# Linear attention in a hybrid decoder trunk: the chunk state of four heads packed into one 64-column block

## The chip, the cores and the metric

One core of one Trainium2 chip. The time is the device time of one execution in microseconds; three runs of the kernel before gave 1186.64, 1187.30 and 1189.42 us, median 1187.3. The profile is of one execution of its own, which took 1187.23 us.

## The reference

Two layers over 512 tokens of 1024 channels. Each layer normalises, projects to four mixers (latent attention, gated linear attention, block attention, a gated recurrence), concatenates, projects back, and runs a SwiGLU network of 2816 hidden channels. The change lies in the gated linear attention: four heads, keys of 32 and values of 64 channels, eight chunks of 64 tokens.

```
b = cumsum(log_sigmoid(a_low @ w_a2 + b_a2) / 16)        # in each chunk
att     = (qf * exp(b - b_last/2)) @ (kf * exp(b_last/2 - b)).T   # 64x64, causal
o_intra = att @ vf
d_state = (kf * exp(b_last - b)).T @ vf                  # 32x64 for head and chunk
state   = exp(b_last) * state + d_state                  # from chunk to chunk
o_inter = (qf * exp(b)) @ state_before
y       = rms_norm(o_intra + o_inter) * silu(g)
```

## The kernel before

Activations lie channels by tokens, 128 x 512 a tile. The dense products run in split single precision: each weight tile and each activation is cut into a high and a low part (`whi`, `wlo`, `xhi`, `xlo`), and a product is three matmuls of 128 x 128 by 128 x 512 (`mm3`). Their outputs are the PSUM tiles `pd` (channels by tokens) and `pt` (tokens by channels). A weight tile comes by DMA into `raw`, ScalarE copies it to `whi`, VectorE or GpSimd subtracts to give `wlo` (`load_split`). Layer 1's mixer weights are split during layer 0's feed-forward and kept in DRAM (`ahead`).

The program is first recorded as a list of operations. A planner in the kernel (`Recorder.schedule`) then lists them in one order by priority, due time and its own cost figures, gives out buffer slots, and that order is emitted; each engine works through its own in that order. `gate` and `also` add a predecessor, or buffers to be had at once, to what is recorded inside them; they bear on the plan alone, and the waits on the chip come from the data. `packed(n)` divides an operation's planned cost by n. `unbroken` makes a run of matmuls start only when the inputs of all are there, and go out in one piece. The dense products have the lowest priority (50), so they fill TensorE whenever nothing else is due.

The linear attention is in two functions. `gla_gates` makes the decays `dcy`, the gated `qt`, `kt`, `qh` (in `gq`'s buffer) and `kh`, the scores `ps_a` (four heads, each 32 rows of the array, four PSUM banks), their masked form `am`, and `khT`, keys by channels. `gla_outputs` does the rest. The state before the change has 256 columns: 128 rows are four heads of 32 channels, columns are four heads of 64 values, and only the four diagonal blocks of 32 x 64 are used. `st` is eight such blocks in four tiles, set to zero by GpSimd. For each pair of chunks, two matmuls (64 rows each, `ps_d`) give the whole 128 x 256 product, and for each chunk and head VectorE adds one 32 x 64 block to the decayed block before (`scalar_tensor_tensor`, 28 in a layer with the first chunk's copies). For each pair of heads, `ps_og` collects eight matmuls of the scores (128 rows, 64 columns of the array, two heads beside one another) and then seven of 128 x 128 state columns by 64 tokens of `qh`, where the zeros in `st` keep the heads apart. ScalarE copies and squares each of the two `ps_og`. A float32 matmul stands in the trace as two instructions, so that 7 matmuls are 14 rows, 16 are 32.

In the profile all recorded operations carry line 397, so tiles are told apart by name.

Of the kernel before, what the change touches and what calls it, by code (L numbers as in the profile page):

```python
# [15 lines left out]
ALU = mybir.AluOpType  # L16
# [3 lines left out]
P = 128  # L20
# [4 lines left out]
QT = S // P  # L25
# [4 lines left out]
NCHUNK = S // CH  # L30
# [370 lines left out]
def trunk_kernel(ctx: ExitStack, tc: tile.TileContext, io):  # L401
    nc = tc.nc
    R = Recorder(nc)
    pe, act, dve, pool, sp = R.pe, R.act, R.dve, R.pool, R.sp
# [4 lines left out]
    def t512(group, dtype=F32, name="t", shape=(S,)):  # L409
        return R.buf("sbuf", group, shape, dtype, name)  # L410
# [4 lines left out]
    def psum(group, name="ps"):  # L415
        return R.buf("psum", group, (S,), F32, name)

    def f(v):
        return v.bitcast(F32)

    def mm(out, l, r, start, stop, **kw):
        return pe.matmul(out, l, r, start=start, stop=stop, skip_group_check=True, **kw)
# [88 lines left out]
    def load_split(ap, group="w", key=None, issue=None):  # L511
        if key in ahead:
            with prio(P_LOAD):
                n = ap.shape[-1]
                hi, lo = t512(group, F32R, "whi", (n,)), t512(group, F32R, "wlo", (n,))
                chain = loads.setdefault(group, [])
                with also(lo), gate(turn["att" if group == "att" else "w"], *chain[-6:-5]):
                    first_ = sp.dma_start(f(hi), ahead[key][0])
                with gate(first_):
                    chain.append(sp.dma_start(f(lo), ahead[key][1]))  # L520
            return hi, lo
        with prio(P_LOAD):
            n = ap.shape[-1]
            raw = t512("raw", F32, "raw", (n,))
            chain = loads.setdefault(group, [])
            with gate(*chain[-6:-5]):
                chain.append((issue or sp).dma_start(raw, ap))
            hi, lo = t512(group, F32R, "whi", (n,)), t512(group, F32R, "wlo", (n,))
            with also(lo):
                act.copy(hi, raw)  # L530
            dve.tensor_sub(lo, raw, f(hi))
        return hi, lo

    class Weights:
# [5 lines left out]
        def block(self, i):  # L540
            if i // 4 != self.at:
                self.at = i // 4
                c = slice(self.at * S, min((self.at + 1) * S, self.n))
                self.w = load_split(self.ap[:, c], self.group, (self.key, self.at))
            c = slice(i % 4 * P, (i % 4 + 1) * P)
            return self.w[0][:, c], self.w[1][:, c]
# [20 lines left out]
    def with_x(k):  # L567
        if k == 0:
            first[0] += [load_split(io["w_in0"][0, 0][:, P:])]
        else:  # L570
            first.append([load_split(io["w_in0"][0, k])])
# [29 lines left out]
    def rstd(ps, n, dim):  # L601
        v, y, t, r = (tiny(name=c)[:, :n] for c in "vytr")
        dve.tensor_scalar(v, ps, 1.0 / dim, EPS, op0=ALU.mult, op1=ALU.add)
        pool.tensor_tensor(y, v, negh[:, :n], op=ALU.pow)
        dve.scalar_tensor_tensor(t, y, -0.5, y, op0=ALU.mult, op1=ALU.mult)
        dve.tensor_mul(t, t, v)
        dve.scalar_tensor_tensor(r, t, 1.5, y, op0=ALU.add, op1=ALU.mult)
        return r
# [365 lines left out]
        return att, khT, qh, dcy, last  # L974

    def gla_outputs(v, att, khT, qh, dcy, last):
        st = []
        with gate(last):
            for _ in range(NCHUNK // 2):
                t = t512("seq", name="st", shape=(2, 256))  # L980
                pool.memset(t, 0.0)
                st += [t[:, 0], t[:, 1]]
        for c0 in range(0, NCHUNK - 1, 2):
            pds = {c: psum("m", "ps_d")[:, :256] for c in (c0, c0 + 1) if c < NCHUNK - 1}
            with unbroken():
                for c, pd in pds.items():
                    r = slice(64 * (c % 2), 64 * (c % 2) + 64)
                    with also(*pds.values()), packed(len(pds)):
                        mm(pd, khT[r, (c // 2) * P:(c // 2 + 1) * P], v[c // 2][r, :], True, True,
                           tile_position=(64 * (c % 2), 0))  # L990
            for c, pd in pds.items():
                for h in range(4):
                    hr, hv = slice(32 * h, 32 * h + 32), slice(64 * h, 64 * h + 64)
                    if c == 0:
                        dve.tensor_copy(st[1][hr, hv], pd[hr, hv])
                    else:
                        dve.scalar_tensor_tensor(st[c + 1][hr, hv], st[c][hr, hv], dcy[hr, c, :], pd[hr, hv],
                                                 op0=ALU.mult, op1=ALU.add)
        os, sqs = [], []
        for p in range(2):  # L1000
            po = psum("m", "ps_og")
            with unbroken():
                for t, hh in ((t, hh) for t in range(QT) for hh in range(2)):
                    tt = slice(t * P, (t + 1) * P)
                    h = 2 * p + hh
                    with packed(2, 19.0):
                        mm(po[64 * hh:64 * hh + 64, tt], v[t][:, h * 64:(h + 1) * 64], att[h][:, tt], t == 0, False)
            for c in range(1, NCHUNK):
                cc = slice(c * CH, (c + 1) * CH)
                mm(po[:, cc], st[c][:, p * P:(p + 1) * P], qh[:, cc], False, c == NCHUNK - 1)  # L1010
            o, sq = t512("seq", name="og"), t512("seq", name="sqg")
            act.copy(o, po)
            act.activation(sq, po, AF.Square)
            os.append(o)
            sqs.append(sq)
        pn = psum("m", "ps_gn")
        for p in range(2):
            for t in range(QT):
                i = 2 * (p * QT + t)
                mm(pn[:, i:i + 2], sqs[p][:, t * P:(t + 1) * P], hsel, True, True)  # L1020
        return os, rstd(pn[:, :16], 16, 64)
# [94 lines left out]
    for l in range(L):  # L1116
# [29 lines left out]
        for what in ORDER:  # L1146
            if what == "v":
                dense_tm([io["w_tm"][l, 0, c] for c in range(4)], nrm, ev_v, "v")
                with prio(9):
                    gla = gla_outputs(gv, *gla)  # L1150
                    gla_end = R.ops[-1]
            elif what == "qk":
                dense_tm([io["w_tm"][l, 1, c] for c in range(4)], nrm, ev_qk, "qk")
            else:
                i = 2 * ("rx", "sg", "rg").index(what)
                fm[what] = [scaled(dense_fm(wf[i + m], nrm, f"fm{i + m}"), nrm, what) for m in range(2)]
# [29 lines left out]
        last = l == L - 1  # L1186
# [9 lines left out]
        for half in range(2):  # L1196
# [16 lines left out]
            with prio(P_DENSE):  # L1213
# [15 lines left out]
                if tail:  # L1229
                    c0 = (KT - tail) * HH * P  # L1230
                    ws = [load_split(io["w_fo"][l, half][:, c:min(c + S, KT * HH * P)], "h")
                          for c in range(c0, KT * HH * P, S)]
                    for q in range(2):
                        c = slice(256 * q, 256 * q + 256)
# [119 lines left out]
```

## Time and profile before

| | |
|---|---|
| median of three runs | 1187.3 us |
| profiled execution | 1187.23 us |
| its span, first to last instruction | 1185.5 us |
| around the span | 1.7 us |
| mean granted TensorE clock | 0.996 |
| busy: TensorE, VectorE, ScalarE, GpSimd | 1168.1, 684.9, 531.6, 232.8 us |
| `ps_d` instructions on TensorE | 28, in 7 pieces |
| `ps_og` instructions on TensorE | 64 of scores, 56 of states |
| state steps on VectorE | 48 steps and 8 copies |

A timeline row gives the start, the time until the last of the merged instructions ends, the engine, the operation with its output and inputs, the stationary tile as rows x columns, the moving operand, and how many instructions are merged. Matmuls are pipelined, so the rows overlap: what a matmul takes of TensorE is the distance between starts, not its duration.

### The profile page before, as it was taken

What the parts mean: (1) busy time and instruction counts of PE and PEld (TensorE: products, weight loads), DVE (VectorE), ACT (ScalarE), POOL (GpSimd) and SP (SyncE); (2) the same over time, 40 slices, a digit from 0 to 9 for tenths busy, and PEclk for the clock granted to TensorE, in tenths of its full rate; (3) what the DMA queues carried; (4) which work ended last, traced back from release to release, by engine and by line L of the source; (5) the groups of instructions that cost most, each with busy time, mean ns of one, the idle gap of its engine ahead of it and who ended that gap; (6) DMA issues with size and microseconds to landing.
All of it is one profiled execution on the core that took longest, in us unless ns stands there. A gap on an engine that the chain in (4) does not pass through costs nothing.

```text
span 1185.5 us, 16334 instructions
## 1 busy us (share of the span) xinstructions
PE 1168.1 (99%) x5568; PEld 963.1 (81%) x5568; DVE 684.9 (58%) x1249; ACT 531.6 (45%) x977; POOL 232.8 (20%) x217
## 2 busy tenths in 40 slices
PE   9999999999999999999999999999999999999996
PEld 6788878788888888888878788888888888888886
DVE  6867688776654456555523765777545433445422
ACT  6545876654443344434422477455433222333331
POOL 4524354460100000022204302206100000000011
PEclk9999999999999999999999999999999999999999
DMA  6322204258676777666795235643233333333312
GB/s 220 111 63 67 72 19 143 80 171 283 227 235 211 242 255 237 222 207 204 256 331 161 79 116 169 195 143 104 93 100 96 97 98 98 98 98 98 95 48 71
DMA packets 101618, 175.25 MB, mean 148 GB/s; under 512 B 11296, under 2 KB 21920, under 8 KB 101536
## 3 DMA queue, kind: packets, MB, share of 16 engines
q1 hardware_dynamic: 100704, 173.58, 46.0%
q8 instruction: 44, 0.72, 0.3%
q10 hardware_dynamic: 832, 0.63, 0.2%
q14 instruction: 38, 0.31, 0.1%
HBM read 139.04 MB, written 35.13 MB: 147 GB/s over the span
## 4 chain that ended last, share of the span: by engine, by line
PE 95%; DMA 1%; ACT 1%; DVE 1%; issue 1%; POOL 0%; POOLq 0%; SPq 0%; DVEq 0%; ACTq 0%
PE pd L397 77%; PE pt L397 8%; PE ps_s L397 2%; PE ps_pt L397 1%; PE ps_o L397 1%; PE ps_q L397 1%; PE ps_og L397 1%; DVE wlo L397 1%; PE ps_g L397 1%; PE ps_d L397 0%; DMA raw<-w_fm 0%; DMA wlo<-ahead 0%; DMA x<-xT 0%; ACT whi L397 0%; PE ps_k L397 0%
## 5 line engine op out<-in xcount | busy, mean ns | idle before, releaser
L397 ACT CAST whi<-raw 128x512 fp32r<-128x512 f32 (+2 forms) x330 | 201.5, 613 | 419.1 <-PE pd L397 376.7
L397 PE MATMUL pd<-xhi,wlo 128*128 128x512 f32 x896 | 350.1, 391 | 1.1 <-DMA wlo<-ahead 1.1
L397 PE MATMUL pd<-xlo,whi 128*128 128x512 f32 x896 | 350.6, 392 | 0.1
L397 PE MATMUL pd<-xhi,whi 128*128 128x512 f32 x896 | 349.0, 391 | 1.2 <-ACT whi L397 1.2
L397 DVE TENSOR_TENSOR wlo<-raw,whi 128x512 fp32r<-128x512 f32 (+2 forms) x282 | 211.8, 754 | 189.5 <-ACT whi L397 178.4
L397 PEld LDWEIGHTS pd<-xhi,wlo 128*128 128x128 f32 x896 | 168.3, 188 | 37.0 <-DMA wlo<-ahead 1.6
L397 PEld LDWEIGHTS pd<-xhi,whi 128*128 128x128 f32 x896 | 168.3, 188 | 37.0 <-ACT whi L397 2.5
L397 PEld LDWEIGHTS pd<-xlo,whi 128*128 128x128 f32 x896 | 168.2, 188 | 35.7 <-issue 1.5
L397 PE MATMUL pd<-hsh,whi 128*128 128x512 f32 (+1 forms) x374 | 141.1, 377 | 0.0
L397 PE MATMUL pd<-hsh,wlo 128*128 128x512 f32 (+1 forms) x374 | 141.0, 377 | 0.0
L397 PE MATMUL pd<-hsl,whi 128*128 128x512 f32 (+1 forms) x374 | 141.0, 377 | 0.0
L397 POOL TENSOR_TENSOR sq<-sq 128x512 f32<-128x512 f32 x35 | 51.1, 1460 | 352.0 <-ACT sq L397 349.9
L397 POOL TENSOR_TENSOR wlo<-raw,whi 128x512 fp32r<-128x512 f32 (+2 forms) x48 | 62.7, 1310 | 118.6 <-ACT whi L397 108.7
L397 PEld LDWEIGHTS pd<-hsh,wlo 128*128 128x128 f32 x374 | 70.3, 188 | 12.9
L397 PEld LDWEIGHTS pd<-hsh,whi 128*128 128x128 f32 x374 | 70.3, 188 | 12.9
L397 PEld LDWEIGHTS pd<-hsl,whi 128*128 128x128 f32 x374 | 70.3, 188 | 12.8
L397 DVE TENSOR_TENSOR x<-x,pd 128x512 f32<-128x512 f32 (+1 forms) x66 | 43.3, 668 | 51.0 <-PE pd L397 50.8
L397 POOL TENSOR_TENSOR plo<-praw,phi 128x512 fp32r<-128x512 f32 (+1 forms) x15 | 19.8, 1322 | 250.8 <-ACT phi L397 137.1
L397 DVE TENSOR_TENSOR fu<-pd,rbc 128x512 f32<-128x512 f32 x44 | 30.4, 691 | 52.3 <-PE pd L397 49.7
L397 DVE TENSOR_TENSOR fg<-pd,rbc 128x512 f32<-128x512 f32 x44 | 30.4, 690 | 40.8 <-PE pd L397 39.3
L397 PE MATMUL pt<-whi,xlo 128*128 128x512 f32 x128 | 51.0, 398 | 0.0
L397 PE MATMUL pt<-wlo,xhi 128*128 128x512 f32 x128 | 50.9, 398 | 0.0
(258 smaller groups left out, 1568.3 us busy)
## 6 DMA issues: line engine op xcount, KB each, us to landing
raw<-w_gu SPq DMA_DIRECT2D x176, 256.0 KB, 2.7
raw<-w_fo SPq DMA_DIRECT2D x88, 256.0 KB, 2.7
ahead<-phi SPq DMA_DIRECT2D x54, 256.0 KB, 3.2
ahead<-plo SPq DMA_DIRECT2D x54, 256.0 KB, 3.3
whi<-ahead SPq DMA_DIRECT2D x54, 256.0 KB, 2.7
wlo<-ahead SPq DMA_DIRECT2D x54, 256.0 KB, 3.2
x<-xT SPq DMA_DIRECT2D x16, 256.0 KB, 5.0
raw<-w_fm SPq DMA_DIRECT2D x16, 256.0 KB, 2.6
```

Of the source, the lines that this page charges most:

```text
L397: op.fn(*[r(a) for a in op.args], **{k: r(v) for k, v in op.kw.items()})
```

## The change

`st` becomes one tile of eight chunks by 64 columns, rows being the four heads' channels, so that each head holds only its own block and nothing has to be zero. The memsets go. The chunk products are made per head: 28 matmuls of 64 rows by 32 columns of the array (`tile_position` of row 0 or 64, column 0, 32, 64 or 96), even chunks into one PSUM bank and odd chunks into another, all in one unbroken run that starts after `khT` and all four value tiles. The recurrence takes the four heads in one VectorE instruction of 128 x 64, seven in a layer. The outputs of both pairs of heads are one unbroken run: 16 score matmuls as before, and then for each chunk four matmuls of 32 rows by 64 columns, one for each head. Last, in `load_split`, the planned copy of a weight tile to `whi` gets the DMA of the load before it as a further predecessor.

```diff
-            with also(lo):
+            with also(lo), gate(*chain[-2:-1]):
                 act.copy(hi, raw)
...
     def gla_outputs(v, att, khT, qh, dcy, last):
-        st = []
-        with gate(last):
-            for _ in range(NCHUNK // 2):
-                t = t512("seq", name="st", shape=(2, 256))
-                pool.memset(t, 0.0)
-                st += [t[:, 0], t[:, 1]]
-        for c0 in range(0, NCHUNK - 1, 2):
-            pds = {c: psum("m", "ps_d")[:, :256] for c in (c0, c0 + 1) if c < NCHUNK - 1}
-            with unbroken():
-                for c, pd in pds.items():
-                    r = slice(64 * (c % 2), 64 * (c % 2) + 64)
-                    with also(*pds.values()), packed(len(pds)):
-                        mm(pd, khT[r, (c // 2) * P:(c // 2 + 1) * P], v[c // 2][r, :], True, True,
-                           tile_position=(64 * (c % 2), 0))
-            for c, pd in pds.items():
+        st = t512("seq", name="st", shape=(NCHUNK, 64))
+        pds = [psum("m", "ps_d") for _ in range(2)]
+        with gate(last), unbroken():
+            for c in range(NCHUNK - 1):
+                r = slice(64 * (c % 2), 64 * (c % 2) + 64)
                 for h in range(4):
-                    hr, hv = slice(32 * h, 32 * h + 32), slice(64 * h, 64 * h + 64)
-                    if c == 0:
-                        dve.tensor_copy(st[1][hr, hv], pd[hr, hv])
-                    else:
-                        dve.scalar_tensor_tensor(st[c + 1][hr, hv], st[c][hr, hv], dcy[hr, c, :], pd[hr, hv],
-                                                 op0=ALU.mult, op1=ALU.add)
-        os, sqs = [], []
-        for p in range(2):
-            po = psum("m", "ps_og")
-            with unbroken():
-                for t, hh in ((t, hh) for t in range(QT) for hh in range(2)):
-                    tt = slice(t * P, (t + 1) * P)
-                    h = 2 * p + hh
-                    with packed(2, 19.0):
-                        mm(po[64 * hh:64 * hh + 64, tt], v[t][:, h * 64:(h + 1) * 64], att[h][:, tt], t == 0, False)
+                    hc = slice(c // 2 * P + 32 * h, c // 2 * P + 32 * h + 32)
+                    with also(*pds), packed(8):
+                        mm(pds[c % 2][32 * h:32 * h + 32, c // 2 * 64:c // 2 * 64 + 64], khT[r, hc],
+                           v[c // 2][r, h * 64:(h + 1) * 64], True, True, tile_position=(64 * (c % 2), 32 * h))
+        for c in range(NCHUNK - 1):
+            pd = pds[c % 2][:, c // 2 * 64:c // 2 * 64 + 64]
+            if c == 0:
+                dve.tensor_copy(st[:, 1], pd)
+            else:
+                dve.scalar_tensor_tensor(st[:, c + 1], st[:, c], dcy[:, c, :], pd, op0=ALU.mult, op1=ALU.add)
+        pos = [psum("m", "ps_og") for _ in range(2)]
+        with unbroken():
+            for t in range(QT):
+                tt = slice(t * P, (t + 1) * P)
+                for h in range(4):
+                    with also(*pos), packed(2, 19.0):
+                        mm(pos[h // 2][64 * (h % 2):64 * (h % 2) + 64, tt], v[t][:, h * 64:(h + 1) * 64], att[h][:, tt],
+                           t == 0, False)
             for c in range(1, NCHUNK):
                 cc = slice(c * CH, (c + 1) * CH)
-                mm(po[:, cc], st[c][:, p * P:(p + 1) * P], qh[:, cc], False, c == NCHUNK - 1)
+                for h in range(4):
+                    hr = slice(32 * h, 32 * h + 32)
+                    with packed(4):
+                        mm(pos[h // 2][64 * (h % 2):64 * (h % 2) + 64, cc], st[hr, c], qh[hr, cc], False, c == NCHUNK - 1,
+                           tile_position=(32 * h, 64 * (h % 2)))
+        os, sqs = [], []
+        for po in pos:
             o, sq = t512("seq", name="og"), t512("seq", name="sqg")
```

## Rows read from the trace of the kernel before

**Rows 1.** The page: busy time by engine (share, instructions), and the chain by engine.

```profile
PE 1168.1 (99%) x5568; PEld 963.1 (81%) x5568; DVE 684.9 (58%) x1249; ACT 531.6 (45%) x977; POOL 232.8 (20%) x217
PE 95%; DMA 1%; ACT 1%; DVE 1%; issue 1%; POOL 0%; POOLq 0%; SPq 0%; DVEq 0%; ACTq 0%
```

**Rows 2.** Timeline, TensorE, layer 1: one `ps_d` piece between dense matmuls.

```profile
656.13 0.39 PE L397 MATMUL ps_q<-cqh,wlo 128*128 128x512 f32 x1
656.36 0.40 PE L397 MATMUL ps_q<-cqh,whi 128*128 128x512 f32 x1
656.68 0.70 PE L397 MATMUL ps_d<-gv,khT 64*128 64x256 f32 x4
...
657.65 0.40 PE L397 MATMUL ps_q<-cqh,wlo 128*128 128x512 f32 x1
```

**Rows 3.** Timeline, TensorE, layer 1: the last `ps_d` pieces and both `ps_og`.

```profile
665.12 0.39 PE L397 MATMUL pd<-xhi,whi 128*128 128x512 f32 x1
...
666.07 0.50 PE L397 MATMUL pd<-xlo,whi 128*128 128x512 f32 x1
666.50 0.70 PE L397 MATMUL ps_d<-gv,khT 64*128 64x256 f32 x2
667.13 1.10 PE L397 MATMUL ps_og<-am,gv 128*64 128x128 f32 x16
668.15 1.77 PE L397 MATMUL ps_og<-gq,st 128*128 128x64 f32 x14
669.74 0.47 PE L397 MATMUL ps_kr<-krsh,selr 128*128 128x512 f32 x1
670.14 1.09 PE L397 MATMUL ps_og<-am,gv 128*64 128x128 f32 x16
...
672.75 0.47 PE L397 MATMUL ps_kr<-krsl,selr 128*128 128x512 f32 x1
673.07 0.28 PE L397 MATMUL ps_gn<-hsel,sqg 128*128 128x2 f32 x2
```

**Rows 4.** Timeline, TensorE, layer 0: the double `ps_d` piece; where `ps_og` begins and ends.

```profile
75.67 0.39 PE L397 MATMUL pd<-xhi,whi 128*128 128x512 f32 x1
75.99 1.13 PE L397 MATMUL ps_d<-gv,khT 64*128 64x256 f32 x8
...
77.39 0.40 PE L397 MATMUL pd<-xhi,wlo 128*128 128x512 f32 x1
...
81.18 0.40 PE L397 MATMUL pd<-xhi,whi 128*128 128x512 f32 x1
...
87.39 0.28 PE L397 MATMUL ps_gn<-hsel,sqg 128*128 128x2 f32 x2
```

**Rows 5.** Timeline, TensorE, layer 0: the scores `ps_a`, four row tiles at once.

```profile
56.28 0.39 PE L397 MATMUL pt<-whi,xlo 128*128 128x512 f32 x1
56.59 1.17 PE L397 MATMUL ps_a<-qt,kt 32*128 32x128 f32 x32
57.70 0.50 PE L397 MATMUL pt<-wlo,xhi 128*128 128x512 f32 x1
58.03 0.40 PE L397 MATMUL pt<-whi,xhi 128*128 128x512 f32 x1
```

**Rows 6.** The same up to 56.69; and `ps_a` by tile (duration min/median/max, ns).

```profile
56.59 0.39 PE L397 MATMUL ps_a<-qt,kt 32*128 32x128 f32 x4
...
L397 PE MATMUL ps_a<-qt,kt x64: 270/270/372, 56.6 to 634.7; 32*128 32x128 f32 x64
```

**Rows 7.** VectorE groups by shape: busy us, mean ns, idle before with releasers.

```profile
L397 DVE SCALAR_TENSOR_TENSOR st<-st,dcy,ps_d 32x64 f32<-32x64 f32 x48 | 13.3, 278 | 1.7 <-PE ps_d L397 0.4
L397 DVE TENSOR_TENSOR wlo<-raw,whi 128x512 fp32r<-128x512 f32 x277 | 208.5, 755 | 186.0 <-ACT whi L397 174.9 <-DMA ahead<-phi 3.6 <-DMA praw<-w_fm 2.4
```

**Rows 8.** The `ps_og` tile's instructions on ScalarE; weight copies, from the page.

```profile
L397 ACT COPY og<-ps_og x4: 585/585/586, 85.7 to 673.0; 128x512 f32<-128x512 f32 x4
...
L397 ACT CAST whi<-raw 128x512 fp32r<-128x512 f32 (+2 forms) x330 | 201.5, 613 | 419.1 <-PE pd L397 376.7
```

## The prediction

> **What bounds the kernel now.** I read the page first. TensorE is busy for 1168.1 of 1185.5 us, and the chain that ended last runs through it for 95% of its length; VectorE, ScalarE and GpSimd have slack [rows 1]. At most 17.4 us of the span is TensorE's idle time, much of it at the two ends. So this kernel's time is the sum of what its matmuls take of TensorE, and what the change is worth is read from the distances between starts on TensorE's timeline. I then took the timeline around the tiles `ps_d` and `ps_og`, where dense matmuls stand on either side, and looked for the nearest operations to the new ones among the small tiles. A wait that appears on another engine counts only where TensorE runs out of dense work in its written order.
>
> **What the old matmuls take.** A dense matmul takes 0.23 us, the distance from 656.13 to 656.36 [rows 2]. A `ps_d` piece of four instructions pushes the next-but-one dense start from 656.36 to 657.65, 1.29 us with one dense matmul between; less two dense steps, the piece takes 0.83. Layer 1 has two such pieces apart. Then come a third, a last one of two instructions, and both `ps_og`: from 665.12 to 673.07 are 7.95 us with four dense matmuls, so 7.03 [rows 3]. Layer 1 together: 8.69. In layer 0 the double piece takes 77.39 - 75.67 - 0.46 = 1.26, the single pieces before and after it 0.83 each, and from 81.18 to 87.39 are 6.21 us with one dense matmul and three half as wide, so 5.63 [rows 4]. Layer 0 together: 8.55. The sum that the change can work on is 17.24 us.
>
> **What the new matmuls take.** First the step from one start to the next round of starts, each time the busy time less one instruction's own. Scores, 128 moving columns on 64 stationary ones, two heads side by side: (1.10 - 0.27) / 7 = 0.118 us. Old state product, 64 moving on 128 stationary columns, one at a time: (1.77 - 0.28) / 13 = 0.115 [rows 3]. `ps_d`, 256 on 128, two at a time: (1.13 - 0.38) / 3 = 0.25 [rows 4]. `ps_a`, 128 on 128, four at a time: (1.17 - 0.27) / 7 = 0.129 [rows 5]. The step goes with the larger of the two column counts, about 0.12 for 128, whether one, two or four tiles run. The old state product therefore paid for its 128 stationary columns, half of them zeros. The new shapes are 64 moving columns on 32 (`ps_d`) and on 64 (`ps_og`); the larger is 64, so I take 0.06. No row has this shape, nor eight tiles at once. Bounds are below.
>
> Rounds: 28 chunk products are 56 instructions; with eight tiles that is 7 rounds, 0.42 us. The state products are also 28, on four tiles, 14 rounds, 0.84 us. The 32 score instructions stay: 15 steps of 0.118 and the 0.19 that lies between the last start and the first state product (1.02 - 0.83), 1.96 [rows 3]. Going from dense work to tiles and back costs what is left over: 1.29 - 8 x 0.129 = 0.26 for `ps_a` [rows 5], 0.26 for the double `ps_d` piece [rows 4], 0.33 for the single one [rows 2]; I take 0.30 for each of two groups. New total for a layer: 0.72 + 3.10 = 3.82, for both 7.64. Saved: 17.24 - 7.64 = 9.6 us. Of this some 2 us is fewer changes of mode (four groups instead of eleven pieces in both layers, 0.30 each), the rest the smaller products.
>
> **Bounds of the step.** At best issue vanishes and the step falls by a tenth: 21 rounds in a layer, 0.3 us in all. At worst, tiles start no closer than `ps_a`'s mean: 32 starts in 0.90, 0.029 apart [rows 5]; 112 new instructions are then 3.25 instead of 1.26 in a layer, 4.0 us in all. I take the even rounds because the first four `ps_a` lie together in 0.39 us although each takes 0.372 [rows 6]: they start within 0.02 us of each other, so 0.029 is 0.12 shared by four and not a spacing.
>
> The Trainium skill ("TensorE: Matmul & The Clock Gate", section "Wait — 56ns, not 53.3ns?") says that starts never come closer than about 25 ns however few columns move, which speaks against cutting into 28 small products. By that floor the 112 starts would take 2.8 us a layer, and the saving would be 6.5. The row of four starts within 0.02 us shows no such floor between tiles [rows 6]; whether it holds between starts on one tile no row can tell, and there it would not bind.
>
> **Edits with nothing on the path.** VectorE: 28 state steps a layer become 7 of the same 64 columns, at 0.278 us, so 5.8 us less a layer [rows 7]. TensorE's dense matmuls covered them; nothing is gained, and what is late next is the same dense stream. The memsets go from GpSimd, which is idle 80% [rows 1]. ScalarE's two copies of 0.585 us and two squares now follow both groups at once instead of the first half lying beside the second's matmuls [rows 8]: two of eight PSUM banks stay held about 1.2 us longer, hidden behind dense work in the other banks; if that cover is gone, at most 1.2 a layer.
>
> The planned gate on the weight copy costs nothing: the load before is issued earlier on the same queue, and the copies wait 376.7 us in total for TensorE to free tiles, not for data [rows 8]. It can only change the order of the plan.
>
> **Waits added.** The first group now needs all four value tiles, the second the whole recurrence. TensorE works in order, so behind a waiting group stand all dense matmuls, and the span's end waits for them. The recurrence is 7 x 0.278 = 1.95 us, and VectorE's `wlo` of 0.755 may lie between [rows 7]. The planner puts dense matmuls in front for that time, as it did for the old steps. I take 0; one `wlo` not foreseen in each layer would be 1.5 us. The planner also orders everything after layer 0's values anew; TensorE's present idle time sets the scale, and I allow 3 us of either sign, taking 0.
>
> **Sum.** 1187.23 - 9.6 = 1177.6 us, against the profiled execution's own time (its span of 1185.5 and 1.7 around it); the median of the runs, 1187.3, is 0.1 above that.
>
> **Rivals.**
> Starts, not columns, set the price: the 0.029 of `ps_a`'s mean holds for smaller work too. For it: never does a row of the trace show more than 32 tile instructions in 0.90 us. Against it: rows 6. Saving 5.6, time 1181.6. Chance 0.15.
>
> The gain comes back as waiting: VectorE is behind the plan when the second group is due, and TensorE stands until the seventh step ends. For it: VectorE is 58% busy and the group is now one piece, where the first half could start before. To eat 4.8 us a layer it takes six `wlo` in front of the steps (6 x 0.755 = 4.5). Against it: VectorE has 21 steps less. Time about 1187. Chance 0.08.
>
> The tiles do not run beside each other, and it gets slower. Heads 0 and 2 use the same 64 columns of the array, even and odd chunks the same 32; and heads 0 and 1 write one PSUM bank from different rows. If every instruction waits for the last at the 0.115 of the old state product, a layer needs 112 x 0.115 = 12.9 instead of 1.26: 23.2 more in both, 1200.8 us. It decides from a mean distance of (1.26 + 4.8) / 112 = 0.054 us on. For it: no row has row and column tiles together. Against it: `ps_a` shares all columns between four row tiles, the scores share a bank between two column tiles, and both overlap. Chance 0.06.
>
> **How the numbers follow.** My forecast has 0.67; 0.04 is for a plan that falls out better than 1174.5. Its own range is the step's gain of 0.3 and 3 us of reordering below, the same above with half a microsecond of waits: 1174.5 to 1181. The range to hold 8 in 10 takes in the first rival and some waiting: 1174.5 to 1183. What can be told from no change is 0.2%, 2.4 us: faster means under 1184.9. Faster holds the forecast, the better plan and the first rival, 0.86; same is mostly the waiting, 0.08; slower the serial tiles, 0.06.
>
> **What would show it.** `ps_d` should be one piece of 56 instructions, about 0.7 us between dense starts; `ps_og` 32 score instructions followed by 56 that span some 0.85 us. The busy time of 56 state products over their mean duration tells the rounds: 14 of 0.06 for the forecast, 56 x 0.029 = 1.6 us for the first rival, over 3 us for the third. Before the second group TensorE should show no idle time put down to `st`. TensorE's waits elsewhere should stay within 3 us of today's. I am wrong if the two groups take as forecast and the span does not fall by 6 us or more, for then the plan has paid it away; or if the groups themselves take more than 6 us a layer.

## The result, and the profile after

The changed kernel takes 1178.2 us, median of four runs (1176.2 to 1179.86), beside 1186.97 for the kernel before: ratio 0.992, 95% interval 0.9904 to 0.9936. Forecast: 1177.6. The ratio makes 9.5 us (7.6 to 11.4), the two medians lie 8.8 apart. The profiled execution took 1177.24 us with a span of 1175.4, 10.1 less than before. One of the six executions of `f5_other_order` below took 2366.86 us, in a slow state, and its figures are those of the other five.

The page of the changed kernel, busy time by engine and the chain by engine:

```profile
PE 1158.3 (99%) x5708; PEld 958.9 (82%) x5708; DVE 675.2 (57%) x1220; ACT 530.0 (45%) x976; POOL 215.7 (18%) x196
...
PE 95%; DMA 2%; DVE 1%; issue 1%; ACT 0%; POOL 0%; POOLq 0%; SPq 0%; DVEq 0%; ACTq 0%
```

TensorE has 140 instructions more than in [rows 1] and is busy 9.8 us less. Span less busy time is 17.1 us, where it was 17.4. So TensorE did not wait less: it worked less. All but 0.3 of the 10.1 us lies there. The mean granted clock was 0.994 instead of 0.996, so the lower clock took some 2 us more than before (0.002 x 1175), and the new order of everything else must have given about as much back; that part was not read apart.

Where in TensorE's work, the timeline of both groups in layer 0 of the changed kernel shows (columns as ahead: start, time to the end of the last merged instruction, engine, line, operation, stationary tile, moving operand, count):

```profile
77.38 0.39 PE L397 MATMUL pd<-xhi,wlo 128*128 128x512 f32 x1
77.69 0.79 PE L397 MATMUL ps_d<-gv,khT 64*32 64x64 f32 x56
78.42 0.50 PE L397 MATMUL pd<-xhi,whi 128*128 128x512 f32 x1
78.75 0.39 PE L397 MATMUL pd<-xlo,whi 128*128 128x512 f32 x1
...
86.81 0.40 PE L397 MATMUL pd<-xhi,wlo 128*128 128x512 f32 x1
87.13 1.97 PE L397 MATMUL ps_og<-am,gv 128*64 128x128 f32 x32
89.03 1.04 PE L397 MATMUL ps_og<-gq,st 32*64 32x64 f32 x56
90.00 0.87 PE L397 MATMUL ps_pt<-cst,p 128*128 128x128 f32 x6
```

As in the prediction, a group costs the distance from the dense start before it to the one that is dense again, less the dense steps between. `ps_d`: 78.75 - 77.38 = 1.37, less two steps of 0.23, is 0.91 us; it stands for the seven pieces of before [rows 2 to 4]. `ps_og`: 90.00 - 86.81 = 3.19, less one step, is 2.96 us, for what was the rest of the 8.69 (layer 1) and 8.55 (layer 0) [rows 3, 4]. One layer now takes 0.91 + 2.96 = 3.87 us. Layer 1 has the same distances to within 0.01 us (659.33 to 660.70, 666.06 to 669.25). Saved: 17.24 - 2 x 3.87 = 9.5 us.

The tile view of the changed kernel, `st` on VectorE (instructions; duration min/median/max in ns; first and last start):

```profile
L397 DVE SCALAR_TENSOR_TENSOR st<-st,dcy,ps_d x12: 264/280/282, 79.4 to 665.2; 128x64 f32<-128x64 f32 x12
L397 DVE COPY st<-ps_d x2: 224/224/225, 79.2 to 660.5; 128x64 f32<-128x64 f32 x2
```

128 rows take what 32 took (278 ns in [rows 7]), so 12 steps replace 48. The last one of layer 1 ends at 665.5, 0.9 us before the group begins and 2.8 before its first state product; no idle time of TensorE is put down to `st`. Elsewhere TensorE's waits have changed places, not their sum. Of the whole span, TensorE's longest waits (line, what for, total us, times, longest):

```profile
PE pd L397 <- DMA wlo<-ahead: 2.5, 1, 2.5
PE ps_rbc L397 <- DVE r L397: 1.7, 1, 1.7
PE pd L397 <- ACT whi L397: 1.3, 2, 0.8
PE pd L397 <- ACT yah L397: 1.2, 1, 1.2
```

The first was 1.1 us in the kernel before, which instead waited 1.9 us for `bkh` and 1.1 for `ych`, both gone here.

### The profile page after: what moved, and what is told of

It reads as the page before. It is cut to its first block, busy times and chain, and to the rows that moved or that the text cites. A ratio compares the mean times of both kernels' runs of the same rounds, so it can differ in the third digit from the quotient of the medians.

```text
span 1175.4 us, 16547 instructions
## 1 busy us (share of the span) xinstructions
PE 1158.3 (99%) x5708; PEld 958.9 (82%) x5708; DVE 675.2 (57%) x1220; ACT 530.0 (45%) x976; POOL 215.7 (18%) x196
## 4 chain that ended last, share of the span: by engine, by line
PE 95%; DMA 2%; DVE 1%; issue 1%; ACT 0%; POOL 0%; POOLq 0%; SPq 0%; DVEq 0%; ACTq 0%
PE pd L397 78%; PE pt L397 8%; PE ps_s L397 2%; PE ps_pt L397 2%; PE ps_o L397 1%; PE ps_q L397 1%; DMA raw<-w_fo 1%; PE ps_g L397 1%; PE ps_og L397 0%; DMA wlo<-ahead 0%; DMA xd<-x 0%; PE ps_ssq L397 0%; PE ps_k L397 0%; DMA x<-xT 0%; PE ps_v L397 0%
## 5 line engine op out<-in xcount | busy, mean ns | idle before, releaser
L397 DVE TENSOR_TENSOR wlo<-raw,whi 128x512 fp32r<-128x512 f32 (+2 forms) x286 | 215.0, 754 | 193.7 <-ACT whi L397 181.8
L397 POOL TENSOR_TENSOR wlo<-raw,whi 128x512 fp32r<-128x512 f32 (+2 forms) x44 | 56.4, 1282 | 109.9 <-ACT whi L397 109.1
L397 POOL TENSOR_TENSOR plo<-praw,phi 128x512 fp32r<-128x512 f32 (+1 forms) x13 | 16.3, 1256 | 270.1 <-ACT phi L397 124.3
L397 PE MATMUL pt<-whi,xhi 128*128 128x512 f32 x128 | 50.7, 396 | 0.0
```

Of the source, the lines that this page charges most:

```text
L397: op.fn(*[r(a) for a in op.args], **{k: r(v) for k, v in op.kw.items()})
```

## The experiments

Theory S (starts): the gain is the 9.5 us of TensorE starts, and each part gives its share wherever it is made. Theory O (order): TensorE's work is cheaper by that much, but what arrives depends on the order that the planner makes of everything behind it.

### One part alone, in both layers

`e1_chunk_products` takes only the chunk products in eight tiles and keeps four state steps a chunk, the zero-filled `st` and the old outputs:

```diff
-                        mm(pd, khT[r, (c // 2) * P:(c // 2 + 1) * P], v[c // 2][r, :], True, True,
-                           tile_position=(64 * (c % 2), 0))
...
+                        mm(pds[c % 2][32 * h:32 * h + 32, c // 2 * 64:c // 2 * 64 + 64], khT[r, hc],
+                           v[c // 2][r, h * 64:(h + 1) * 64], True, True, tile_position=(64 * (c % 2), 32 * h))
```

> The kernel before with the chunk products alone in the new 64-row by 32-column tiles, one run; state of 256 columns, memsets, 28 steps on VectorE and the outputs as before. My theory (time is TensorE's starts): the pieces of ps_d took 2.9 us in layer 0 and about 3.2 in layer 1, the new run takes 0.91 as in the changed kernel, so 4.3 us less in both layers together: ratio near 0.996. Rival (the gain is mostly in the output products, where 128 stationary columns were half zeros): under 1 us less. Rival (the 28 steps on VectorE, with less time before the outputs, hold TensorE up): no gain or slower, with TensorE idle before ps_og put down to st.

`e2_outputs` takes only the outputs as one group with per-head state products:

```diff
-                mm(po[:, cc], st[c][:, p * P:(p + 1) * P], qh[:, cc], False, c == NCHUNK - 1)
...
+                        mm(pos[h // 2][64 * (h % 2):64 * (h % 2) + 64, cc], st[c][hr, h * 64:(h + 1) * 64], qh[hr, cc], False, c == NCHUNK - 1,
+                           tile_position=(32 * h, 64 * (h % 2)))
```

> The kernel before with the outputs alone as one run of 32 score instructions and 56 state products of 32 rows by 64 columns, which read the diagonal blocks of the old 256-column state; chunk products, memsets and 28 steps as before. My theory: the two halves took 5.6 us a layer, the new run 3.0, so 5.2 us less in both: ratio near 0.9956, and together with the chunk products alone the whole of the change. Rival (the second group waits for the whole recurrence, 28 steps of 0.278 us): 1 to 3 us of that come back as TensorE idle before ps_og, put down to st.

Both were slower than before: 1194.95 us (1.0073, 1.006 to 1.0085) and 1193.19 (1.0055, 1.0041 to 1.0069), beside 1186.42. Yet the new groups themselves are as cheap as in the whole change; here the timeline of the first, then of the second:

```profile
74.09 0.39 PE L397 MATMUL pd<-xhi,wlo 128*128 128x512 f32 x1
74.41 0.79 PE L397 MATMUL ps_d<-gv,khT 64*32 64x64 f32 x56
```

```profile
85.37 1.97 PE L397 MATMUL ps_og<-am,gv 128*64 128x128 f32 x32
87.27 1.04 PE L397 MATMUL ps_og<-gq,st 32*64 32x64 f32 x56
88.24 0.50 PE L397 MATMUL ps_q<-cql,whi 128*128 128x512 f32 x1
```

The loss is some 70 us later, in layer 0's attention. The view of windows for 150 to 235 us (stretch, its length; busy time and instructions of PE, PEld, DVE, ACT, POOL; granted clock; DMA share; GB/s), of the kernel before, of the first, the second, and the changed kernel:

```profile
150.00:235.00 85.00, 80.98 (x417) 66.64 (x417) 71.98 (x181) 56.89 (x135) 38.54 (x42) 0.98 0.26 82
```

```profile
150.00:235.00 85.00, 75.25 (x373) 60.22 (x372) 66.30 (x170) 49.58 (x121) 27.51 (x33) 0.96 0.24 77
```

```profile
150.00:235.00 85.00, 75.79 (x367) 61.10 (x366) 66.62 (x168) 49.47 (x121) 28.18 (x34) 0.92 0.24 75
```

```profile
150.00:235.00 85.00, 82.02 (x405) 67.76 (x404) 70.86 (x149) 53.91 (x119) 42.52 (x43) 0.98 0.31 95
```

TensorE stands 9.8 and 9.2 us there instead of 4.0 (waits of up to 2.0 us for `ych`, `bkh`, `ydl`, `pth`). In the first, no dense matmul starts between 162.4 and 178.2 us, where only the attention's own chain is walked; before the change that stretch was shorter, from 169.5 to 179.0. Why less dense work was left there is not shown. And the clock is lower, 0.96 and 0.92. Over the whole span, idle time (span less busy) is 24.1 and 22.0 us against 17.4; busy time, 1169.1 and 1169.4, is above the 1168.1 of before, although the two groups together, measured as above from dense start to dense start, take 3.4 and 4.8 us less (13.8 and 12.4 in both layers, where it was 17.2). For `e1` this is less than the 4.3 that its chunk products save, since its plan scatters the old state products in small pieces among dense matmuls. Three of them, from the timeline of layer 0:

```profile
80.28 0.73 PE L397 MATMUL ps_og<-gq,st 128*128 128x64 f32 x4
...
81.61 0.62 PE L397 MATMUL ps_og<-gq,st 128*128 128x64 f32 x4
...
82.83 0.63 PE L397 MATMUL ps_og<-gq,st 128*128 128x64 f32 x4
```

The busy time that this leaves unexplained, 1.0 + 3.4 = 4.4 and 1.3 + 4.8 = 6.1 us, is put down to the lower clock; the mean granted clock, 0.993 and 0.991 where it was 0.996, makes 0.003 x 1193 = 3.6 and 0.005 x 1191 = 6.0 of it. So e1 is -3.4 + 6.7 + 4.4 = +7.7, its span's growth (1193.2 against 1185.5); e2 is -4.8 + 4.6 + 6.1 = +5.9. Theory S fails on the time of both. The loss lies where theory O has it, and neither run shows TensorE idle before `ps_og`, which a rival of each expected. But both also keep the 28 steps on VectorE, which these two runs do not tell apart from the order.

### The whole change, in one layer

`f1_layer1_only` calls the new function in layer 1 and the old one in layer 0; `f2_layer0_only` has `l == 0` in the same place.

```diff
-                    gla = gla_outputs(gv, *gla)
+                    gla = (gla_outputs if l == 1 else gla_outputs_before)(gv, *gla)
```

> The change in layer 1 alone, layer 0 as before. In layer 1 TensorE never runs out of dense work, before or after. My theory (there every microsecond of matmul starts saved reaches the end): the two groups take 3.9 us instead of 8.7, so 4.8 less, 1181.6 against a before of 1186.4, and layer 0's mixers with the same idle of TensorE as before (1.9 before ps_s, 1.1 before the last block of outputs). Rival (all of the gain and loss is an accident of the written order): anything from 1180 to 1195.

> The change in layer 0 alone, layer 1 as before. Theory of two limits (in layer 0 the attention heads on VectorE and ScalarE end last while dense work runs out, so the order decides what of the saving is kept): layer 0 ends as in the changed kernel, some 10 us earlier than before, half of which is late dense work; the time is that of the changed kernel plus the 4.8 us of layer 1, 1183. Rival (matmul starts alone): 1186.4 - 4.7 = 1181.7. Rival (accident): 1180 to 1195.

Layer 1 alone: 1182.18 beside 1186.84 (0.9961, 0.9948 to 0.9974), 4.7 less (3.1 to 6.2), where the starts are worth 8.69 - 3.87 = 4.8. The plan ahead of layer 1, attention of layer 0 included, is nearly the old one (its last `ps_o` starts at 221.0, before at 222.7). This is the clean reading of theory S. Layer 0 alone: 1179.96 (0.9944, 0.9922 to 0.9965), 6.9 less, for starts worth 4.7; the 2.2 more lie within the interval (2.6 us either way). Both forecasts for it, 1183 and 1181.7, are above what was measured, and the first lies outside the interval (1177.6 to 1182.7). The last `ps_o` of its layer 0 starts at 210.1.

### The order of the small instructions

`e3_head_by_head` writes both groups head by head, instead of chunk by chunk with the head innermost; nothing else changes. The state products:

```diff
...
-            for c in range(1, NCHUNK):
-                cc = slice(c * CH, (c + 1) * CH)
-                for h in range(4):
+            for h in range(4):
+                for c in range(1, NCHUNK):
+                    cc = slice(c * CH, (c + 1) * CH)
```

> The changed kernel with the same instructions in another order: chunk products and state products head by head instead of chunk by chunk, so that instructions of one head, which use one column strip (chunk products) or one tile (state products), follow each other. My theory (the gain is that tiles run side by side, and the written order decides it): state products go one after the other at 0.058 us, 56 x 0.058 = 3.2 us instead of 0.85, chunk products two at a time, 1.5 us instead of 0.45; 3.5 us a layer, 7 us in both, so some 1185 us, about 1.006 of the changed kernel. Rival (the step is set by columns alone, and TensorE picks its order among tiles by itself): no change, 1178.

1183.55 beside 1186.42 (0.9966, 0.9953 to 0.9979), so 5.5 us of the gain are lost. The timeline of layer 0:

```profile
77.76 1.39 PE L397 MATMUL ps_d<-gv,khT 64*32 64x64 f32 x56
...
89.72 2.94 PE L397 MATMUL ps_og<-gq,st 32*64 32x64 f32 x56
```

0.60 and 1.90 us longer in each layer, 5.0 in all. Most of the 56 state products now start 0.058 us apart, where four started together in that time. Here the written order decided whether tiles ran beside each other: where the next instruction wanted the same tile, the others stood empty. That is the third rival in a milder form, and it shows that the forecast rested on the written order.

### The state steps, and the order of the plan

`e4_steps_by_head` is the changed kernel with four steps of 32 rows for each one of 128. `f3_steps_same_order` issues the same four, but keeps the changed kernel's order of everything else. `f4_steps_other_order` is e4 with a planner margin of 165 instead of 150, which only reorders.

```diff
-                dve.scalar_tensor_tensor(st[:, c + 1], st[:, c], dcy[:, c, :], pd, op0=ALU.mult, op1=ALU.add)
+            for h in range(4):
+                hr = slice(32 * h, 32 * h + 32)
...
+                    dve.scalar_tensor_tensor(st[hr, c + 1], st[hr, c], dcy[hr, c, :], pd[hr], op0=ALU.mult, op1=ALU.add)
```

> The changed kernel with the recurrence again in 28 VectorE instructions of 32 x 64 a layer instead of 7 of 128 x 64. My theory (VectorE lies beside dense matmuls): within 1.5 us of the changed kernel, 1178, TensorE's ps_d and ps_og runs of the same length. Rival (the shorter recurrence is what lets the second run go out in time): 2 to 6 us slower, with TensorE idle before ps_og put down to st.

> The changed kernel planned as it is, but each of the seven state steps goes out as four instructions of 32 x 64, one for each head, so that VectorE does 28 steps in nearly the same written order. It tells apart why the steps by head cost 7.7 us before. Theory of the order (the planner, told of 28 steps, wrote a worse order for layer 0's attention; the steps themselves are covered): within 2 us of the changed kernel, 1178 to 1180. Theory of VectorE's load (21 x 0.278 = 5.8 us more a layer on an engine that is busy for over three quarters of layer 0's attention): 1184 to 1187, with TensorE idle between 140 and 235 us.

> The 28 steps by head as in the run that took 1185.9, with one planner constant changed (the margin added before a due time on TensorE, 165 instead of 150), which writes another order of the same instructions. Theory of the order: several microseconds away from 1185.9, about 1180. Theory of VectorE's load: 1185 to 1187 again.

| kernel | us | beside | ratio (95%) | TensorE busy in 150 to 235 |
|---|---|---|---|---|
| e4 | 1185.91 | 1186.42 | 0.9994 (0.9984 to 1.0005) | 76.80 |
| f3 | 1188.66 | 1186.84 | 1.0014 (1.0004 to 1.0023) | 82.02 |
| f4 | 1179.09 | 1186.84 | 0.9933 (0.9917 to 0.9948) | 80.35 |

f4 against e4: the same instructions, 0.6% apart (some 7 us). So the 28 steps alone do not make e4's loss; its order has a part in it. With margin 165, 28 steps and seven take the same time (f4 0.9933, f5 below 0.9932); with 150 they are 8.8 us apart (e4 0.9994, the changed kernel 0.992). Both forecasts for e4 missed: it is 7.7 us above the changed kernel, and none of TensorE's idle time stands before `ps_og`.

f3 is some 11 us above the changed kernel, beyond either forecast, and here it is VectorE's time: the order was laid out for seven steps, and TensorE waits where the 28 stand in front of what it needs. This happens at the groups, not in 140 to 235 us. TensorE's waits of f3 in 72 to 100 us, and the timeline at the second one:

```profile
PE pd L397 <- DVE kl L397: 2.1, 1, 2.1
PE ps_s L397 <- DVE st L979: 1.8, 1, 1.8
```

```profile
86.97 1.21 DVE L979 SCALAR_TENSOR_TENSOR st<-st,dcy,ps_d 32x64 f32<-32x64 f32 x4
...
88.32 1.09 PE L397 MATMUL ps_s<-kh,qh 128*128 128x128 f32 x3 [1.82 <-DVE st L979]
```

Neither is the second group waiting for its state, the forecast's second rival; before `ps_og` f3 has no idle time of TensorE either. The first waits for `kl`, which stands behind state steps on VectorE. The second, the scores of latent attention, does not read `st`; it goes on as the step of the last odd chunk ends, in layer 1 too, so a wait for the PSUM bank that the odd chunks held would fit, but this was not tested. With two such waits in layer 1 (1.9 and 1.1) they are 6.9 us. They cost twice: the windows of f3 at and after the first two show the clock at half.

```profile
83.00:87.00 4.00, 1.39 (x5) 0.67 (x4) 3.65 (x12) 0.87 (x2) 1.27 (x1) 1.00 0.53 168
87.10:93.70 6.60, 5.38 (x17) 4.72 (x17) 4.73 (x16) 1.08 (x3) 0.00 (x0) 0.50 0.05 17
```

### The gate, and the margin on the two kernels

`e5_no_gate` undoes the further predecessor of the weight copy. `f5_other_order` is the changed kernel with margin 165, `f7_before_other_order` the kernel before with it.

```diff
-            with also(lo), gate(*chain[-2:-1]):
+            with also(lo):
...
-SLACK, RELEASE, COOL, WARM, CARE, SPARE = 150.0, 300.0, 400.0, 4000.0, 1.0, 100.0
+SLACK, RELEASE, COOL, WARM, CARE, SPARE = 165.0, 300.0, 400.0, 4000.0, 1.0, 100.0
```

> The changed kernel without the gate on the copy of a weight tile. My theory (the gate is free: the load before lands first anyway, and the order of TensorE, VectorE and SyncE is the same without it): 1178, within 2 us. Rival (the gate keeps the weight tiles in turn and is part of the gain): 3 us slower or more, with TensorE waiting for whi or wlo.

> The changed kernel with the planner's margin of 165 instead of 150: the same instructions in another order. Theory of the order (what layer 0's attention keeps of the saving depends on the order written): more than 2 us away from 1178, likely slower, 1180 to 1183, all of it in TensorE's idle time and lower clock between 140 and 235 us. Theory of starts alone: within 1.5 us of 1178.

> The kernel before with the planner's margin of 165 instead of 150, nothing else. It shows how much the written order moves a kernel without the change. Theory of the order: several microseconds from 1186.6, either way. Theory of starts alone: within 1.5 us.

Beside 1186.11: e5 1176.59 (0.9924, 0.9912 to 0.9936), the changed kernel's time within the interval, and the order of TensorE's, VectorE's and SyncE's instructions is the same with and without the gate: it is free. f5 1177.82 (0.9932, 0.992 to 0.9944): no change. f7 1184.85 (0.9991, 0.9983 to 1.0): 1.3 less. Both are against what theory O expected. Not every new order costs: the changed kernel keeps its gain under both margins, and e4 under the second alone. e1 and e2 were not planned with another margin.

### Scores in four tiles

`f6_scores_64` goes on where the rows point: the score products are now the larger part of the second group, 1.90 of 2.96 us, and half of each 128 x 128 score block is masked zeros. They become 64 x 64 tiles by chunk, into four PSUM banks by parity of the chunk, and the copies to `og` take half a bank each.

```diff
-                        mm(pos[h // 2][64 * (h % 2):64 * (h % 2) + 64, tt], v[t][:, h * 64:(h + 1) * 64], att[h][:, tt],
-                           t == 0, False)
...
+                        mm(pos[c % 2][h // 2][64 * (h % 2):64 * (h % 2) + 64, c // 2 * 64:c // 2 * 64 + 64],
+                           v[c // 2][r, h * 64:(h + 1) * 64], att[h][r, cc], c < 2, False,
+                           tile_position=(64 * (c % 2), 64 * (h % 2)))
```

> The changed kernel with the score products too in small tiles: 32 of 64 rows by 64 columns (even chunks in rows 0 to 63, odd ones in 64 to 127, which leaves out the products with the masked zeros), four tiles at once, even and odd chunks in banks of their own, the outputs copied in halves. By the step of 0.058 us for 64 columns: 16 rounds, 0.93 us instead of 1.9, so 1.0 us less a layer, and 1176 if the order were kept. The order will move, so the time may be 2 to 4 us either side; what counts is the distance between the dense starts around the group: 2.0 us instead of 3.0. Rival (row tiles that write the same partitions hold each other up): the scores take 1.9 us or more again.

1174.41 beside 1186.11 (0.9906, 0.9892 to 0.9921), below both kernels, and 2.2 us below e5, which stands beside the same 1186.11 (the two intervals overlap a little). The timeline of layer 0:

```profile
87.72 0.40 PE L397 MATMUL pd<-xhi,whi 128*128 128x512 f32 x1
88.05 1.21 PE L397 MATMUL ps_og<-am,gv 64*64 64x64 f32 x64
89.19 1.04 PE L397 MATMUL ps_og<-gq,st 32*64 32x64 f32 x56
90.16 0.33 PE L397 MATMUL ps_pt<-cst,p 128*128 128x128 f32 x1
```

Twice as many instructions start in 1.14 us instead of 1.90: the group is 2.21 instead of 2.96, 1.5 us in both layers.

## Why the prediction was right

**The main term.** 9.5 us against 9.6 forecast, and f1 shows it alone: 4.7 measured for 4.8. `ps_og` was 2.96 for 3.10: the last of 14 rounds starts (1.04 - 0.22) = 0.82 after the first, a step of 0.82 / 13 = 0.063 for the 0.06 taken, and changing over cost less than 0.30. Start by start, the rounds of four follow 0.058 apart but for the first distance, 0.107. `ps_d` was 0.91 for 0.72: its 56 starts take 0.57 (0.79 - 0.22), where six steps of 0.06 would be 0.36. Its first four rounds of eight are even, 0.24 us for 32 starts; the other 24 are staggered over 0.31, and why is not known. So four tiles keep the even rounds, eight did not quite. The two misses, -0.14 and +0.19 a layer, nearly cancel, and that is luck.

**The edits at nothing.** The gate is nothing (e5). In the changed kernel no group waits for `st`. VectorE's relief was put at nothing since dense matmuls covered the steps. With margin 165 that holds (f4 and f5). With 150, the margin of the changed kernel, it does not: 28 steps cost 8.8 us (e4) or, in the order laid out for seven, some 11 (f3). The merged steps save no TensorE time themselves, but in this plan the gain is not kept without them; the prediction did not have that, and the time did not show it.

**The rivals.** Starts 0.029 apart: 56 state products would span 1.6 us and span 1.04. Waiting for `st`: no run shows TensorE idle before `ps_og`; in f3 VectorE is behind the plan as this rival had it, but TensorE stands elsewhere. Serial tiles: refuted for the order as written; e3 shows how near a part of it lay, 5.0 us.

**What failed without showing in the time.** "The planner also orders everything after layer 0's values anew; TensorE's present idle time sets the scale, and I allow 3 us of either sign". The scale is wrong. e1 ended 7.7 + 3.4 = 11.1 us and e2 5.9 + 4.8 = 10.7 us above what their starts allow, e4 some 7 above f4. The changed kernel kept its gain with an order that served it: the last `ps_o` of layer 0 starts at 211.6 instead of 222.7 us, with 3.0 us of idle time in 150 to 235 (4.0 before). Nothing in the forecast told this order from e4's, so that its term of 0 came true was luck. An honest upper end would have been near 1188, and "same" would have had more than 0.08. TensorE's idle time was the wrong scale since a new order made idle time that was not there (6.7 and 4.6 us more in e1 and e2), and the lower clock took about as much again (4.4 and 6.1). A smaller slip: 1177.6 less 0.3 and 3 is 1174.3, not 1174.5.

**Open.** Which decision of the planner starves e1, e2 and e4 is not settled, nor whether the 28 steps do it. All three have them in layer 0. The runs with the new groups there and seven steps all kept what their own starts left them (f2, f5, e5, f6, and e3 less its 5.0); with 28, only f4 did. That the order alone made e1 and e2 slow is argued, not shown. The early start of latent attention's queries is not it: `ps_q` begins at 69.4 us in the changed kernel (87.5 before), but at 71.6 in e1 and 69.6 in e4 too. Nor was it tried what the changed kernel would gain without its one new loss, the wait of 2.5 us for `wlo<-ahead` at the layer's boundary. Its windows there (columns as above):

```profile
585.00:588.00 3.00, 0.47 (x4) 0.05 (x2) 0.95 (x2) 0.00 (x0) 0.00 (x0) 1.00 0.92 315
588.60:591.80 3.20, 3.20 (x9) 2.53 (x8) 0.75 (x1) 1.24 (x2) 1.04 (x1) 0.50 1.04 384
592.00:595.00 3.00, 3.00 (x18) 2.56 (x17) 0.00 (x0) 0.62 (x1) 0.03 (x1) 1.00 0.90 306
```

In the stretch after the wait the clock is at half and eight matmuls start, 0.43 us apart where 0.23 is usual: 8 x 0.20 = 1.6 us on top of it.

## What to carry to other kernels

In the shapes of this case, small products in tiles paid by the larger of their moving and stationary columns, so try to cut both and let neighbours in the queue use different tiles; read the price as the distance between dense starts, whose sum came out here to 2%. On a planned kernel a saving on the bound engine need not arrive at the end, so read TensorE's busy time in the next dependent stretch before and after, and allow for the scatter of orders (some 10 us here), not for today's idle time. An edit that takes work from an engine off the path can still decide whether a plan keeps the gain, as the state steps did here under one margin and not under the other. To measure one term, change it where nothing behind it is short of work, as in layer 1 here.

## What the runs showed of the hardware

Starts on different tiles come very close. The timeline of the changed kernel, cut off at 77.74 us, shows how many `ps_d` instructions have begun 0.05 us after the first:

```profile
77.69 0.28 PE L397 MATMUL ps_d<-gv,khT 64*32 64x64 f32 x7
```

Over the whole group the mean distance is 0.57 / 55 = 0.010 us on eight tiles, and 0.82 / 55 = 0.015 on four.

The Trainium skill ("TensorE: Matmul & The Clock Gate", section "Wait — 56ns, not 53.3ns?") gives about 25 ns as the least distance between starts; an estimate by it for the 56 is 1.4 us. The trace disagrees between tiles, with 0.57 us for the 56. Within one tile nothing here comes near it: most starts on one tile in e3 are 0.058 us apart.

The clock fell after short idle times, though not each time. In the changed kernel's layer 0, TensorE is busy half of 4 us, with waits of 1.2 and 0.8, and the granted clock then goes from 2.4 to 1.2 GHz:

```profile
168.00:172.00 4.00, 1.97 (x11) 1.16 (x10) 3.94 (x12) 2.67 (x9) 1.28 (x1) 1.00 0.00 0
172.20:175.40 3.20, 3.20 (x12) 2.71 (x11) 2.85 (x12) 2.75 (x8) 0.73 (x1) 0.50 0.66 188
```

The same stretch went either way: in the profiles of e5 and f2, whose TensorE has the changed kernel's order there, it is busy for 1.99 and 1.96 of the same 4 us, and the clock is 1.00 in the whole of 150 to 235 us.
